# A shorter second key search, a 16-bit decoding, and GpSimd taken out of the low parts of U

## The chip, the cores and the metric

The kernel runs on one core of one Trainium2 chip. The metric is device time in microseconds (us), the median of several executions; lower is better. A core has TensorE (PE, matrix products; its weight loads are listed as PEld), VectorE (DVE), ScalarE (ACT), GpSimd (POOL), and SyncE (SP), which here issues the DMAs. Each engine works through its own queue in order and waits at semaphores for the others.

## The reference, cut to what matters

The model is a hybrid block (stick-breaking attention, a linear recurrence and an FFN) on 256 tokens of width 1024, followed by two layers of attention and an expert FFN, PEER. The change lies in PEER, which each of the two layers runs once:

```python
PEER_HEADS, PEER_NKEYS, PEER_TOPK = 8, 128, 16
q = (xc @ wq).reshape(PEER_CHUNK, PEER_HEADS, 2, half)
sc = jnp.einsum('chpd,hpnd->chpn', q, sub_keys)
s1, i1 = lax.top_k(sc[:, :, 0], PEER_TOPK)
s2, i2 = lax.top_k(sc[:, :, 1], PEER_TOPK)
cand = (s1[..., :, None] + s2[..., None, :])   # 16 x 16 sums
cidx = (i1[..., :, None] * PEER_NKEYS + i2[..., None, :])
top_s, pos = lax.top_k(cand, PEER_TOPK)        # over the 256 sums
eidx = jnp.take_along_axis(cidx, pos, axis=-1)
g = jax.nn.softmax(top_s, axis=-1)
a = gelu(u[eidx] . xc);  out = sum of (g * a) * v[eidx]
```

There are 16384 experts; u and v have 16384 rows of 1024 each.

## The kernel before, in words

The kernel does not gather the chosen rows. It multiplies all of U with all 256 tokens, block by block (128 blocks of 128 experts), and keeps the gelu of the products, `S`; it builds the gates of the chosen experts with one-hot matrices and multiplies them in; then it multiplies the gated `S` with all of V. In `peer` this is, in the order of the code:

- `query` (8 heads): W blocks are loaded, split and multiplied; ScalarE evicts the queries to `QT`.
- `topk(hd, t)` for 8 heads and two halves of the tokens (`t`): key scores by TensorE into `g`, copied to `sc`; then three searches for the best 16 on VectorE (`top16`, L1432 to L1436: the best 8, their places, take them out, the next 8, their places): one in each key half (128 scores), and, after the outer sum `cand` (L1451), one over the 256 sums, which gives values `tv` and places `pos`.
- `decode(t)`: a place is split into a = pos >> 4 and b = pos & 15; which key a or b stands for is found with a comparison against 0..15 (L1469), a product with the key numbers `ixf` (L1472) and a reduction (L1473), over 32 x 16 numbers of 32 bits, eight times for each half (two j, four x). Then the softmax: `gg` is the shifted `tv` (L1477), ScalarE takes its Exp (L1478), VectorE sums and divides; TensorE transposes, ScalarE and VectorE write `ID` and `GD`.
- `ublock(b)`: a block of U, 512 KB, comes by DMA into `raw` (3 buffers). A 32-bit number is split into a high part that TensorE takes as it is and a low part: ScalarE writes `hi` (L221), and `lo` = raw - hi (L222) is written by VectorE or GpSimd. There are two buffers of `hi`, two of `lo` and one more, `lo3`, for every third block. 24 matmuls follow (L1387, L1388 with `hi`, L1390 with `lo`) into one of two banks `a`, and ScalarE evicts it with a gelu (L1393, `S`). `uload` runs two blocks ahead.
- For the first `TURN` = 46 blocks, steps of `topk` and `decode` are put between the blocks: `steps()` yields 64 times, 14 of them during the queries and 50 over the 46 blocks.
- Afterwards `gstep` builds one-hots E of 8 tokens (L1527 to L1529) and multiplies (L1542), and the later blocks go on; then the V blocks (L1571).

Who makes `lo` is set by `ONPOOL`: every even block below 46 on GpSimd, 23 in a layer. The split is done by these lines of `load_split`:

```python
for a, b, r in parts:
    nc.scalar.activation(a, r, AF.Copy)
    (sub or nc.vector).tensor_sub(b, r, a.bitcast(F))
```

A scheduler orders each engine's queue by its own model of the times before the kernel is built, so the order on an engine is not that of the code.

Of the kernel before, what the change touches and what calls it, by code (L numbers as in the profile page):

```python
# [8 lines left out]
F = mybir.dt.float32  # L9
FR = mybir.dt.float32r  # L10
BF = mybir.dt.bfloat16
HF = mybir.dt.float16
U32 = mybir.dt.uint32
AF = mybir.ActivationFunctionType
OP = mybir.AluOpType
AX = mybir.AxisListType
# [1322 lines left out]


TURN = 46
ONPOOL = lambda b: b < TURN and b % 2 == 0


def peer(tc, A, K, dump, h, l, X, out):
    nc = tc.nc
    PSUM = bass.MemoryType.PSUM
    V, SC, G, PE = nc.vector, nc.scalar, nc.gpsimd, nc.tensor
    ident = K.ident
    ts = lambda t: slice(t * 128, (t + 1) * 128)  # L1350
    NT = 8

    def on_pool(b):
        return ONPOOL(b)

    with ExitStack() as es:
        pp = es.enter_context(tc.tile_pool(name=f"pp{l}", bufs=1))
# [13 lines left out]
        def uload(b):  # L1371

            def src(raw):
                nc.sync.dma_start(raw, A["peer_u_2"][l, b])

            room = pp.tile([128, 1024], FR, name="lo3", tag="lo3") if b % 3 == 2 else None
            hi, lo = K.load_split(src, 1024, lo=room, sub=G if on_pool(b) else None, halves=False)
            ub[b] = [x.rearrange("p (k e) -> p k e", k=8) for x in (hi, lo)]

        def ublock(b):  # L1380
# [13 lines left out]
            if n:  # L1394
# [4 lines left out]
        tp = tks.enter_context(tc.tile_pool(name=f"tp{l}", bufs=1))  # L1399
        iotaf = tp.tile([128, 128], F, name="iotaf")  # L1400
        G.iota(iotaf, [[1, 128]], base=0, channel_multiplier=0, allow_small_or_imprecise_dtypes=True)
        iota = iotaf[:, 0:16]
        V.tensor_copy(iotah, iotaf)
        QT = tp.tile([128, 8, 2, S], F, name="QT")
        KT = tp.tile([128, 8, 2, 128], F, name="KT")
        nc.scalar.dma_start(KT, A["peer_keys_2"][l])
        tk = [dict(tv=tp.tile([128, 8, 16], F, name=f"tv{t}"), pos=tp.tile([128, 8, 16], U32, name=f"pos{t}"),
                   ix=tp.tile([128, 8, 2, 16], U32, name=f"ix{t}")) for t in range(2)]
# [22 lines left out]
        def top16(v, ix, s, s2):  # L1431
            V.max(v[:, 0:8], s)  # L1432
            V.max_index(ix[:, 0:8], v[:, 0:8], s)
            V.match_replace(s2, v[:, 0:8], s, -3e38)  # L1434
            V.max(v[:, 8:16], s2)
            V.max_index(ix[:, 8:16], v[:, 8:16], s2)  # L1436

        def topk(hd, t):
            d = tk[t]
            w = pg.tile([128, 512], F, name="g", tag="g")  # L1440
            for j in range(2):
                PE.matmul(w[:, j * 128:(j + 1) * 128], lhsT=QT[:, hd, j, ts(t)], rhs=KT[:, hd, j], start=True, stop=True)
            v = tp.tile([128, 2, 16], F, name="v", tag="v", bufs=2)
            sc = tp.tile([128, 2, 128], F, name="sc", tag="sc", bufs=2)
            s2 = tp.tile([128, 256], F, name="s2", tag="s2", bufs=2)
            SC.activation(sc, w[:, 0:256].rearrange("p (j n) -> p j n", j=2), AF.Copy)
            for j in range(2):
                top16(v[:, j], d["ix"][:, hd, j], sc[:, j], s2[:, 0:128])
                yield
            cand = tp.tile([128, 256], F, name="cand", tag="cand", bufs=2)  # L1450
            V.tensor_add(cand.rearrange("p (a b) -> p a b", b=16), v[:, 0].unsqueeze(2).to_broadcast([128, 16, 16]),  # L1451
                         v[:, 1].unsqueeze(1).to_broadcast([128, 16, 16]))
            top16(d["tv"][:, hd], d["pos"][:, hd], cand, s2)
            yield

        def decode(t):
            d = tk[t]
            f = lambda nm: tp.tile([128, 8, 16], F, name=nm, tag=nm)
            u = tp.tile([128, 8, 16], U32, name="u", tag="u")
            ixf = tp.tile([128, 8, 2, 16], F, name="ixf", tag="ixf")  # L1460
            V.tensor_copy(ixf, d["ix"])
            sel = [f(f"sel{j}") for j in range(2)]
            for j in range(2):
                V.tensor_scalar(u, d["pos"], 4 if j == 0 else 15, None, op0=OP.logical_shift_right if j == 0 else OP.bitwise_and)
                pf = f("pf")
                V.tensor_copy(pf, u)
                for x in range(0, 8, 2):
                    oh = tp.tile([128, 32, 16], F, name="oh", tag="oh", bufs=2)
                    V.tensor_tensor(oh, pf[:, x:x + 2].rearrange("p h k -> p (h k)").unsqueeze(2).to_broadcast([128, 32, 16]),  # L1469
                                    iota.unsqueeze(1).to_broadcast([128, 32, 16]), op=OP.is_equal)  # L1470
                    o4 = oh.rearrange("p (h k) a -> p h k a", h=2)
                    V.tensor_mul(o4, o4, ixf[:, x:x + 2, j].unsqueeze(2).to_broadcast([128, 2, 16, 16]))  # L1472
                    V.tensor_reduce(sel[j][:, x:x + 2].rearrange("p h k -> p (h k)"), oh, AX.X, OP.add)  # L1473
                    if x < 6 or j == 0:
                        yield
            gg = f("gg")
            V.tensor_sub(gg, d["tv"], d["tv"][:, :, 0:1].to_broadcast([128, 8, 16]))  # L1477
            SC.activation(gg, gg, AF.Exp)  # L1478
# [5 lines left out]
            for j in range(2):  # L1484
                PE.transpose(w[:, j * 128:(j + 1) * 128], sel[j].rearrange("p h k -> p (h k)"), ident)
            PE.transpose(w[:, 256:384], gg.rearrange("p h k -> p (h k)"), ident)
            twice = lambda x: x.unsqueeze(len(x.shape)).to_broadcast(list(x.shape) + [2])
            SC.activation(ID[:, :, ts(t)], twice(w[:, 0:256].rearrange("p (j t) -> p j t", j=2)), AF.Copy)
            gs = tp.tile([128, 128], F, name="gs", tag="gs")
            SC.activation(gs, w[:, 256:384], AF.Copy, scale=2.0 ** 14)  # L1490
# [12 lines left out]
        done = 0  # L1503
# [150 lines left out]
```

## Time and profile before

| what | value |
|---|---|
| median of 3 runs | 2463.34 us (2461.76 to 2466.64) |
| the profiled execution | 2460.61 us, span 2458.8 us |
| TensorE busy | 2346.7 us, 95% |
| VectorE busy | 1697.5 us, 69% |
| ScalarE busy | 1205.5 us, 49% |
| GpSimd busy | 370.3 us, 15% |
| mean granted clock of TensorE | 0.982 of 2.4 GHz |

Busy times are shares of the whole span, which has many stages. What a stage is bound by is read from its own stretch: how much each engine is busy in it, what TensorE's idle time ended with, and at which clock it ran. 1.00 stands for 2.4 GHz and 0.50 for 1.2 GHz; a mean between them is a mix of the two over the stretch.

### The profile page before, as it was taken

The numbers are of one execution on the slowest core, as the hardware profiler recorded it, in microseconds if no ns is written. First come the engines' busy times: TensorE is split into PE (matmuls) and PEld (weight loads), VectorE is DVE, ScalarE is ACT, GpSimd is POOL, SyncE is SP. The second block draws the span as 40 slices with busy tenths as digits, with TensorE's granted clock in tenths as the row PEclk, the third lists the DMA queues.
The fourth block names the chain that finished last, engine by engine and source line by source line (L and its number), as shares of the span: only waits on it lengthen the run. The fifth ranks groups of instructions, "written<-read, shape, count | busy, mean of one in ns | idle before, by whom it ended". The sixth has DMA issues, their size and how long they took to land.

```text
span 2458.8 us, 43487 instructions
## 1 busy us (share of the span) xinstructions
PE 2346.7 (95%) x17012; PEld 2122.6 (86%) x17012; DVE 1697.5 (69%) x3190; ACT 1205.5 (49%) x2118; POOL 370.3 (15%) x299
## 2 busy tenths in 40 slices
PE   8978989998999999999999999999999999999998
PEld 7877879977799999999888877689999999888886
DVE  4467565557789968886555556779967888556555
ACT  4663554444435445544545454534545554455543
POOL 0065400007304410000000004502430000000000
PEclk9999999998999999999999999999999999999999
DMA  5332146555145454545556565325455555566664
GB/s 176 86 108 76 57 145 185 185 181 164 57 138 164 155 179 157 166 161 188 191 196 191 194 204 179 112 78 168 152 171 165 163 163 178 190 191 196 192 194 146
DMA packets 145637, 389.68 MB, mean 158 GB/s; under 512 B 18731, under 2 KB 49510, under 8 KB 145174
## 3 DMA queue, kind: packets, MB, share of 16 engines
q1 hardware_dynamic: 140070, 375.34, 47.8%
q10 hardware_dynamic: 5360, 11.56, 1.5%
q8 instruction: 133, 2.18, 0.4%
q14 instruction: 74, 0.61, 0.1%
HBM read 385.34 MB, written 1.31 MB: 157 GB/s over the span
## 4 chain that ended last, share of the span: by engine, by line
PE 56%; DVE 14%; issue 2%; ACT 2%; DMA 2%; POOL 0%; ACTq 0%; DVEq 0%; POOLq 0%
PE w L1571 27%; PE a L1387 7%; PE a L1388 7%; PE a L1390 7%; DVE lo L222 3%; PE w L1542 2%; PE a L1304 2%; DVE s L1434 1%; DMA raw<-in_peer_v_dram 1%; DVE oh L1469 1%; ACT hi L221 1%; PE w L1423 1%; PE o L1268 1%; DVE oh L1472 1%; DVE ix L1436 1%
## 5 line engine op out<-in xcount | busy, mean ns | idle before, releaser
L221 ACT ACTIVATE hi<-raw 128x1024 fp32r<-128x1024 f32 (+1 forms) x696 | 709.2, 1023 | 853.1 <-PE w L1571 312.0
L222 DVE TENSOR_TENSOR lo<-raw,hi 128x1024 fp32r<-128x1024 f32 (+1 forms) x610 | 745.7, 1224 | 524.6 <-ACT hi L221 518.9
L1387 PE MATMUL a<-XH,hi 128*128 128x256 f32 x2048 | 505.8, 285 | 8.9 <-ACT S L1393 5.9
L1388 PE MATMUL a<-XL,hi 128*128 128x256 f32 x2048 | 499.9, 282 | 0.0
L1571 PE MATMUL w<-hi,ww 128*128 128x512 f32 x1968 | 488.9, 389 | 4.1 <-ACT ww L226 4.1
L1571 PEld LDWEIGHTS w<-hi,ww 128*128 128x128 f32 x1968 | 368.8, 188 | 83.0 <-ACT ww L226 6.6
L1387 PEld LDWEIGHTS a<-XH,hi 128*128 128x128 f32 x2048 | 391.3, 191 | 12.7 <-ACT S L1393 6.3
L1388 PEld LDWEIGHTS a<-XL,hi 128*128 128x128 f32 x2048 | 391.3, 191 | 0.0
L1390 PE MATMUL a<-XH,lo 128*128 128x256 f32 x2048 | 293.2, 284 | 8.3 <-DVE lo L222 8.3
L1390 PEld LDWEIGHTS a<-XH,lo 128*128 128x128 f32 x2048 | 262.8, 190 | 9.3 <-DVE lo L222 9.1
L1571 PE MATMUL w<-lo,ww 128*128 128x512 f32 x984 | 264.4, 390 | 0.0
L222 POOL TENSOR_TENSOR lo<-raw,hi 128x1024 fp32r<-128x1024 f32 (+1 forms) x86 | 190.6, 2226 | 314.0 <-ACT hi L221 289.1
L173 POOL TENSOR_TENSOR ag<-ag,mhalf 128x1 f32<-128x1 f32 x10 | 9.5, 951 | 1464.0 <-DVE ag L349 1253.0
L1571 PEld LDWEIGHTS w<-lo,ww 128*128 128x128 f32 x984 | 184.2, 188 | 40.3 <-DVE lo L222 2.3
L264 PE MATMUL pj<-XH,hi 128*128 128x256 f32 (+1 forms) x424 | 124.6, 299 | 5.1 <-ACT gs L593 3.3
L266 PE MATMUL pj<-XH,lo 128*128 128x256 f32 (+1 forms) x424 | 117.5, 300 | 4.9 <-DVE lo L222 3.8
L265 PE MATMUL pj<-XL,hi 128*128 128x256 f32 (+1 forms) x424 | 122.1, 293 | 0.0
L227 DVE TENSOR_TENSOR ww<-S,ww 128x256 fp32r<-128x256 f32 x246 | 102.5, 417 | 0.0
L226 ACT ACTIVATE ww<-S 128x256 fp32r<-128x256 f32 x246 | 98.0, 399 | 0.0
L265 PE MATMUL pj<-big,hi 128*128 128x256 f32 x352 | 97.8, 283 | 0.0
L264 PE MATMUL pj<-big,hi 128*128 128x256 f32 x352 | 97.4, 283 | 0.0
L266 PE MATMUL pj<-big,lo 128*128 128x256 f32 x352 | 92.6, 283 | 0.0
(502 smaller groups left out, 3564.3 us busy)
## 6 DMA issues: line engine op xcount, KB each, us to landing
raw<-in_peer_u_dram SPq DMA_DIRECT2D x256, 512.0 KB
raw<-in_peer_v_dram SPq DMA_DIRECT2D x256, 512.0 KB
raw<-in_w_in_dram SPq DMA_DIRECT2D x58, 512.0 KB
raw<-in_w_ffn_in_dram SPq DMA_DIRECT2D x88, 256.0 KB
raw<-in_peer_wq_dram SPq DMA_DIRECT2D x32, 512.0 KB
raw<-in_w_ffn_out_dram SPq DMA_DIRECT2D x22, 512.0 KB
raw<-in_w_o_dram SPq DMA_DIRECT2D x16, 512.0 KB
raw<-in_w_out_dram SPq DMA_DIRECT2D x8, 512.0 KB
```

What stands on the lines that cost most here:

```text
L221: nc.scalar.activation(a, r, AF.Copy)
L222: (sub or nc.vector).tensor_sub(b, r, a.bitcast(F))
L226: self.nc.scalar.activation(hi, xf, AF.Copy)
L227: self.nc.vector.tensor_sub(lo, xf, hi.bitcast(F))
L264: PE.matmul(ps[j], lhsT=wh, rhs=xh(kk), start=kk == 0 and j % per == 0, stop=False)
L265: PE.matmul(ps[j], lhsT=wh, rhs=xl(kk), start=False, stop=False)
L266: PE.matmul(ps[j], lhsT=wl, rhs=xh(kk), start=False, stop=kk == KT - 1 and (j % per == per - 1 or j == len(subs) - 1))
L1304: K.marks["out"] = PE.matmul(po[t][c], lhsT=x[:, k, ts(t)], rhs=w[:, c * 512:(c + 1) * 512], start=f and not i and k == ks[0], stop=e and ...
L1387: PE.matmul(a, lhsT=hi[:, k], rhs=XH[:, k], start=k == 0, stop=False)
L1388: PE.matmul(a, lhsT=hi[:, k], rhs=XL[:, k], start=False, stop=False)
L1390: PE.matmul(a, lhsT=lo[:, k], rhs=XH[:, k], start=False, stop=k == 7)
L1571: K.marks["v"] = PE.matmul(acc[t][:, n], lhsT=x[:, ts(t)], rhs=v[:, n * 512:(n + 1) * 512], start=f, stop=e)
```

## The change

Three things change, all in `peer`. GpSimd makes no `lo` of U any more: `ONPOOL` and `on_pool` are gone, and VectorE makes all of them. The outer sums are cut to 112: the first four keys of one half with all 16 of the other, and the other twelve with the first four; a place is then decoded with a = max(pos >> 4, (pos >> 2) - 12) and b = pos - 16a + 12 max(a - 4, 0). The decoding works on all 8 heads at once, in 16-bit numbers: a comparison and a product over 8 x 16 x 16 = 2048 numbers, then a tree of additions instead of a reduction. `decode` yields 6 times instead of 8, so the steps are 60 and their pace over the blocks is set anew.

```diff
-ONPOOL = lambda b: b < TURN and b % 2 == 0
...
-            hi, lo = K.load_split(src, 1024, lo=room, sub=G if on_pool(b) else None, halves=False)
+            hi, lo = K.load_split(src, 1024, lo=room)
...
+        rank = tp.tile([128, 16, 16], HF, name="rank")
+        V.tensor_copy(rank, iota.unsqueeze(2).to_broadcast([128, 16, 16]))
...
-            cand = tp.tile([128, 256], F, name="cand", tag="cand", bufs=2)
-            V.tensor_add(cand.rearrange("p (a b) -> p a b", b=16), v[:, 0].unsqueeze(2).to_broadcast([128, 16, 16]),
-                         v[:, 1].unsqueeze(1).to_broadcast([128, 16, 16]))
-            top16(d["tv"][:, hd], d["pos"][:, hd], cand, s2)
+            cand = tp.tile([128, 112], F, name="cand", tag="cand", bufs=2)
+            for a, n, k in ((slice(0, 4), 4, 16), (slice(4, 16), 12, 4)):
+                V.tensor_add(cand[:, 16 * a.start:16 * a.start + n * k].rearrange("p (a b) -> p a b", b=k),
+                             v[:, 0, a].unsqueeze(2).to_broadcast([128, n, k]), v[:, 1, 0:k].unsqueeze(1).to_broadcast([128, n, k]))
+            top16(d["tv"][:, hd], d["pos"][:, hd], cand, s2[:, 0:112])
...
-            V.tensor_copy(ixf, d["ix"])
...
+            V.tensor_scalar(u, pos, 4, None, op0=OP.logical_shift_right)
+            V.tensor_scalar(u2, pos, 2, None, op0=OP.logical_shift_right)
+            V.scalar_tensor_tensor(ab[:, 0], u2, -12.0, u, op0=OP.add, op1=OP.max)
+            far, rest = f("far"), f("rest")
+            V.tensor_scalar(far, ab[:, 0], -4.0, 0.0, op0=OP.add, op1=OP.max)
+            V.scalar_tensor_tensor(rest, ab[:, 0], -16.0, pos, op0=OP.mult, op1=OP.add)
+            V.scalar_tensor_tensor(ab[:, 1], far, 12.0, rest, op0=OP.mult, op1=OP.add)
+            yield
             for j in range(2):
-                V.tensor_scalar(u, d["pos"], 4 if j == 0 else 15, None, op0=OP.logical_shift_right if j == 0 else OP.bitwise_and)
-                pf = f("pf")
-                V.tensor_copy(pf, u)
-                for x in range(0, 8, 2):
-                    oh = tp.tile([128, 32, 16], F, name="oh", tag="oh", bufs=2)
-                    V.tensor_tensor(oh, pf[:, x:x + 2].rearrange("p h k -> p (h k)").unsqueeze(2).to_broadcast([128, 32, 16]),
-                                    iota.unsqueeze(1).to_broadcast([128, 32, 16]), op=OP.is_equal)
-                    o4 = oh.rearrange("p (h k) a -> p h k a", h=2)
-                    V.tensor_mul(o4, o4, ixf[:, x:x + 2, j].unsqueeze(2).to_broadcast([128, 2, 16, 16]))
-                    V.tensor_reduce(sel[j][:, x:x + 2].rearrange("p h k -> p (h k)"), oh, AX.X, OP.add)
-                    if x < 6 or j == 0:
-                        yield
+                V.tensor_copy(ixd[:, j], twice(d["ix"][:, :, j]))
+                oh = tp.tile([128, 8, 16, 16], HF, name="oh", tag="oh", bufs=2)
+                V.tensor_tensor(oh, ab[:, j].unsqueeze(2).to_broadcast([128, 8, 16, 16]), rank.unsqueeze(1).to_broadcast([128, 8, 16, 16]),
+                                op=OP.is_equal)
+                yield
+                o4 = oh.rearrange("p h a (k u) -> p (h a) k u", u=2)
+                V.tensor_mul(o4, o4, ixd[:, j].rearrange("p h a u -> p (h a) u").unsqueeze(2).to_broadcast([128, 128, 8, 2]))
+                for n in (8, 4, 2):
+                    V.tensor_add(oh[:, :, 0:n], oh[:, :, 0:n], oh[:, :, n:2 * n])
+                V.tensor_add(sel[j], oh[:, :, 0], oh[:, :, 1])
+                yield
...
-            while done < 64 and done < 14 + (b + 1) * 50 // (TURN - 2):
+            while done < 60 and done < 14 + (b + 1) * 46 // (TURN - 2):
```

How the queues change is shown at three places of the first layer; a row is a line number, an operation, its tiles (numbers tell buffers of a name apart) and its shape. The first is GpSimd's queue from the number row `iotaf` on, before:

```order
L1401 IOTA iotaf 128x128
L222 TENSOR_TENSOR lo<-raw,hi 128x1024
L222 TENSOR_TENSOR lo_7233<-raw,hi 128x1024
L222 TENSOR_TENSOR lo<-raw,hi 128x1024 x2
L222 TENSOR_TENSOR lo_7473<-raw,hi 128x1024
L222 TENSOR_TENSOR lo<-raw,hi 128x1024 x2
L222 TENSOR_TENSOR lo_7720<-raw,hi 128x1024
```

and after:

```order
L1397 IOTA iotaf 128x128
L173 TENSOR_TENSOR ag<-ag,mhalf 128x1
L222 TENSOR_TENSOR big<-raw,big 128x512
L222 TENSOR_TENSOR big<-raw,big 128x256
L222 TENSOR_TENSOR big<-raw,big 128x512
L222 TENSOR_TENSOR big<-raw,big 128x256
L222 TENSOR_TENSOR big<-raw,big 128x512 x2
```

The `lo` of U are gone; the next thing GpSimd does is the layer norm's power and the weights of the second layer (`big`).

The second is VectorE's queue up to the softmax's `gg` of the first token half, before, from a `lo` on:

```order
L222 TENSOR_TENSOR lo<-raw,hi 128x1024
L1461 CAST ixf<-ix_6600 128x256
L1432 MAX tv_6598<-cand 128x8
L1433 MAX_INDEX pos_6599<-tv_6598,cand 128x8
L1434 MATCH_REPLACE s_8293<-tv_6598,cand 128x256
L1432 MAX v<-sc 128x8
L1435 MAX tv_6598<-s_8293 128x8
L1432 MAX v<-sc 128x8
L1433 MAX_INDEX ix_6603<-v,sc 128x8
L1434 MATCH_REPLACE s_8413<-v,sc 128x128
L1436 MAX_INDEX pos_6599<-tv_6598,s_8293 128x8
L1477 TENSOR_TENSOR gg<-tv_6598 128x128
```

and after, from the `lo` ahead of `gg` to the next one:

```order
L222 TENSOR_TENSOR lo_7844<-raw,hi 128x1024
L1433 MAX tv_6600<-s_8373 128x8
L1433 MAX tv_6603<-s_8494 128x8
L1434 MAX_INDEX pos_6601<-tv_6600,s_8373 128x8
L1488 TENSOR_TENSOR gg<-tv_6600 128x128
L1434 MAX_INDEX pos_6604<-tv_6603,s_8494 128x8
L1467 TENSOR_SCALAR u<-pos_6601 128x128
L1468 TENSOR_SCALAR u_8611<-pos_6601 128x128
L222 TENSOR_TENSOR lo<-raw,hi 128x1024
```

Before, `gg` stands twelve rows behind a `lo`, behind the cast `ixf`, and the last head of the second token half (the `sc` rows) is still in its first searches. After, the last search of both halves is nearly done at `gg`, the casts (`ixd`) stand further ahead, and the next `lo` follows four rows later.

The third is VectorE's queue in the decoding, before, around the `lo` that follows the first half's comparisons:

```order
L1469 TENSOR_TENSOR oh<-pf,iotaf 128x512 x2
L1472 TENSOR_TENSOR oh<-oh,ixf 128x512 x2
L1466 CAST pf<-u 128x128
L1473 TENSOR_REDUCE sel_8500<-oh 128x32
L222 TENSOR_TENSOR lo<-raw,hi 128x1024
L1473 TENSOR_REDUCE sel_8500<-oh 128x32
L1461 CAST ixf<-ix_6603 128x256
L1464 TENSOR_SCALAR u<-pos_6602 128x128
L1469 TENSOR_TENSOR oh<-pf,iotaf 128x512 x2
```

and after, at the first wide product:

```order
L222 TENSOR_TENSOR lo<-raw,hi 128x1024
L1482 TENSOR_TENSOR oh<-oh,ixd 128x2048
L1493 TENSOR_TENSOR gg<-gg,sm 128x128
L1478 TENSOR_TENSOR oh<-ab,rank 128x2048
L222 TENSOR_TENSOR lo_7965<-raw,hi 128x1024
L1484 TENSOR_TENSOR oh<-oh 128x8x128
L1482 TENSOR_TENSOR oh<-oh,ixd 128x2048
L1469 SCALAR_TENSOR_TENSOR ab<-u_8849,u 128x128
L222 TENSOR_TENSOR lo<-raw,hi 128x1024
L1484 TENSOR_TENSOR oh<-oh 128x8x64
L1484 TENSOR_TENSOR oh<-oh 128x8x128
```

Before, five or six rows (eight instructions, of 512 numbers most) stand between two `lo` of VectorE, and GpSimd makes the one between. After, every `lo` is here, with one to three wide or small operations between two.

## Rows read from the trace of the kernel before

**Rows 1.** Stretches: us, busy time (x instructions) by engine, PEclk, DMA share, GB/s.

```profile
683.10:864.90 181.80, 170.26 (x1386) 167.98 (x1387) 169.42 (x514) 85.77 (x135) 56.91 (x20) 0.96 0.48 158
1628.70:1811.50 182.80, 171.27 (x1438) 169.17 (x1439) 169.79 (x514) 85.60 (x135) 55.97 (x20) 0.96 0.49 158
683.10:735.00 51.90, 48.79 (x403) 47.47 (x404) 45.21 (x176) 21.93 (x37) 0.21 (x1) 1.00 0.45 150
735.00:788.70 53.70, 53.07 (x455) 52.87 (x454) 53.49 (x232) 28.09 (x44) 24.09 (x9) 1.00 0.55 177
788.70:864.90 76.20, 68.40 (x530) 67.65 (x531) 70.72 (x109) 35.75 (x54) 32.61 (x11) 0.91 0.46 150
1000.00:1100.00 100.00, 99.74 (x1117) 98.12 (x1117) 84.71 (x136) 49.52 (x106) 0.00 (x0) 1.00 0.50 164
```

**Rows 2.** Waits of TensorE, 683 to 865: total us, times, longest us.

```profile
PE a L1390 <- DVE lo L222: 4.2, 2, 2.3
PE a L1387 <- ACT S L1393: 3.0, 1, 3.0
...
PE w L1423 <- ACT hi L221: 1.0, 1, 1.0
```

**Rows 3.** Stretches around slow clock, columns as in rows 1.

```profile
790.00:798.00 8.00, 6.97 (x36) 6.97 (x37) 8.00 (x17) 3.63 (x6) 2.89 (x1) 0.57 0.43 133
820.00:826.00 6.00, 5.58 (x34) 5.58 (x35) 6.00 (x12) 2.32 (x3) 0.00 (x0) 0.72 0.47 175
848.00:852.00 4.00, 4.00 (x23) 4.00 (x23) 1.26 (x2) 0.96 (x2) 0.00 (x0) 0.57 0.85 292
```

**Rows 4.** Timeline: start us, us, engine, line, operation, tiles [idle before <-releaser].

```profile
782.56 3.15 POOL L222 TENSOR_TENSOR lo<-raw,hi 128x1024 fp32r<-128x1024 f32 x1 [2.43 <-ACT hi L221]
783.36 2.50 DVE L1461 CAST ixf<-ix 128x256 f32<-128x256 uint32 x1
785.46 1.28 ACT L1478 ACT_TABLE_LOAD   x1
788.98 0.31 ACT L1478 ACTIVATE gg<-gg 128x128 f32<-128x128 f32 x1 [2.24 <-DVE gg L1477]
789.30 1.28 ACT L1393 ACT_TABLE_LOAD   x1
791.03 0.58 PE L1387 MATMUL a<-XH,hi 128*128 128x256 f32 x1 [2.96 <-ACT S L1393]
...
816.91 2.38 POOL L222 TENSOR_TENSOR lo<-raw,hi 128x1024 fp32r<-128x1024 f32 x1 [2.77 <-ACT hi L221]
817.15 3.22 DVE L222 TENSOR_TENSOR lo<-raw,hi 128x1024 fp32r<-128x1024 f32 x1
```

**Rows 5.** VectorE by form, 735 to 788.7: xcount | busy us, mean ns.

```profile
L222 DVE TENSOR_TENSOR lo<-raw,hi 128x1024 fp32r<-128x1024 f32 x8 | 9.6, 1206 | 0.0
...
L1436 DVE FIND_INDEX8 ix<-v,s 128x8 uint32<-128x128 f32 x18 | 5.0, 282 | 0.0
L1451 DVE TENSOR_TENSOR cand<-v 128x256 f32<-128x256 f32 x9 | 4.9, 543 | 0.0
L1436 DVE FIND_INDEX8 pos<-tv,s 128x8 uint32<-128x256 f32 x11 | 4.5, 415 | 0.0
```

**Rows 6.** VectorE by form, 788.7 to 864.9.

```profile
L222 DVE TENSOR_TENSOR lo<-raw,hi 128x1024 fp32r<-128x1024 f32 x12 | 18.3, 1526 | 0.6 <-issue 0.6
L1472 DVE TENSOR_TENSOR oh<-oh,ixf 128x512 f32<-128x512 f32 x16 | 14.9, 966 | 0.0
L1469 DVE TENSOR_TENSOR oh<-pf,iotaf 128x512 f32<-128x512 f32 x16 | 14.9, 959 | 0.0
L1473 DVE TENSOR_REDUCE sel<-oh 128x32 f32<-128x512 f32 x16 | 10.4, 673 | 0.0
...
L1529 DVE TENSOR_TENSOR E<-E,GD 128x1024 f16<-128x1024 f16 x2 | 1.3, 677 | 0.0
```

**Rows 7.** VectorE by form, 885 to 1100.

```profile
L1396 DVE TENSOR_TENSOR S<-a,S 128x64 f32<-128x64 f32 x2 | 0.4, 215 | 0.0
```

More of the change, by code (lines that the diff above doesn't have):

```diff
@@ L1351, in peer @@
     NT = 8
-    def on_pool(b):
-        return ONPOOL(b)
     with ExitStack() as es:
@@ L1458, in decode @@
             f = lambda nm: tp.tile([128, 8, 16], F, name=nm, tag=nm)
-            u = tp.tile([128, 8, 16], U32, name="u", tag="u")
-            ixf = tp.tile([128, 8, 2, 16], F, name="ixf", tag="ixf")
-            V.tensor_copy(ixf, d["ix"])
-            sel = [f(f"sel{j}") for j in range(2)]
-            for j in range(2):
-                V.tensor_scalar(u, d["pos"], 4 if j == 0 else 15, None, op0=OP.logical_shift_right if j == 0 else OP.bitwise_and)
-                pf = f("pf")
-                V.tensor_copy(pf, u)
-                for x in range(0, 8, 2):
-                    oh = tp.tile([128, 32, 16], F, name="oh", tag="oh", bufs=2)
-                    V.tensor_tensor(oh, pf[:, x:x + 2].rearrange("p h k -> p (h k)").unsqueeze(2).to_broadcast([128, 32, 16]),
-                                    iota.unsqueeze(1).to_broadcast([128, 32, 16]), op=OP.is_equal)
-                    o4 = oh.rearrange("p (h k) a -> p h k a", h=2)
-                    V.tensor_mul(o4, o4, ixf[:, x:x + 2, j].unsqueeze(2).to_broadcast([128, 2, 16, 16]))
-                    V.tensor_reduce(sel[j][:, x:x + 2].rearrange("p h k -> p (h k)"), oh, AX.X, OP.add)
-                    if x < 6 or j == 0:
-                        yield
@@ new lines, in decode @@
+            twice = lambda x: x.unsqueeze(len(x.shape)).to_broadcast(list(x.shape) + [2])
+            pos = d["pos"]
+            u, u2 = (tp.tile([128, 8, 16], U32, name=n, tag=n) for n in ("u", "u2"))
+            ab = tp.tile([128, 2, 8, 16], HF, name="ab", tag="ab")
+            ixd = tp.tile([128, 2, 8, 16, 2], HF, name="ixd", tag="ixd")
+            sel = [f(f"sel{j}") for j in range(2)]
+            V.tensor_scalar(u, pos, 4, None, op0=OP.logical_shift_right)
+            V.tensor_scalar(u2, pos, 2, None, op0=OP.logical_shift_right)
@@ L1486, in decode @@
             PE.transpose(w[:, 256:384], gg.rearrange("p h k -> p (h k)"), ident)
-            twice = lambda x: x.unsqueeze(len(x.shape)).to_broadcast(list(x.shape) + [2])
             SC.activation(ID[:, :, ts(t)], twice(w[:, 0:256].rearrange("p (j t) -> p j t", j=2)), AF.Copy)
```

## The prediction

> **What bounds the kernel now.** I read the page's totals first, then the stretches, then what TensorE waits for, then what those waits rest on. TensorE is busy in nearly all of the span, so only places where it stands still or runs slow can give time back. In each of the two expert layers there is one such place: from the first query projection to the first gating matmul, 683.1 to 864.9 us and 1628.7 to 1811.5 us [rows 1]. The reader is to see TensorE's busy time, its clock and VectorE's busy time together. After that place, from 1000 to 1100, TensorE is busy 99.74 of 100 us although VectorE is busy 84.71 [rows 1]: one `lo` per U block on VectorE with this much beside it holds nobody up. Inside the place TensorE is idle 181.80 - 170.26 = 11.5 us and its clock is 0.96.
>
> The idle time has names [rows 2]: 4.2 us until a `lo` of VectorE, in two waits; 3.0 us until a gelu of ScalarE (`S`), in one wait; the rest, 4.3 us, is the first loads of the queries and the first one-hots E. Behind each of the three long waits the granted clock falls to its half level for a while: 0.57 over 8 us, 0.72 over 6 us, 0.57 over 4 us [rows 3]. That costs 8 x 0.43 + 6 x 0.28 + 4 x 0.43 = 3.4 + 1.7 + 1.7 = 6.8 us more. So 11.5 + 6.8 = 18.3 us of a layer's 181.8 are lost, and 1628.7 to 1811.5 has the same sums (11.5 us idle, clock 0.96). All of it won twice would be 37 us, the ceiling.
>
> What the waits rest on is in the timeline [rows 4]. At 816.91 GpSimd starts a `lo` of 2.38 us; at 817.15 VectorE starts one, and it takes 3.22 us where the same shape has a mean of 1.206 in a stretch where none of its eight was stretched [rows 5]. TensorE waits for exactly this one. At 783.36 a cast of 256 numbers takes 2.50 us, again beside a GpSimd `lo`; five us later ScalarE's Exp has waited 2.24 us for VectorE's `gg`, which stands behind that cast, and ScalarE's queue is in order, so the gelu behind the Exp and its table load (1.28 us) is late and TensorE waits 2.96 us for a free bank. The shift is seen in the means too: between 788.7 and 864.9 `lo` has 1526 ns, the decoding's product and comparison 966 and 959, but the reduction of as many elements 673 [rows 6].
>
> **The change, part by part.** Everything is for one layer; both layers have it.
>
> *GpSimd's 23 `lo` go to VectorE* (20 of them in this place, 9 and 11 in its two later stretches [rows 1]). VectorE pays 20 x 1.206 = 24.1 us. It gets back what the overlap cost it: 12 x (1.526 - 1.206) + 16 x (0.966 - 0.673) + 16 x (0.959 - 0.673) = 3.8 + 4.7 + 4.6 = 13.1 us in the decoding, and 9 x (0.543 - 0.43) + 2.50 - 0.28 = 3.2 us in the search (0.28 is the price of a 128-element operation [rows 5], 0.43 that of two adds of 64 [rows 7]). The Trainium skill, "SBUF — State Buffer", section "Who interferes with whom", says that VectorE and GpSimd share one port pair as a lock, held for a whole instruction, and that the one issued second stops altogether. The 3.22 us beside 1.206 agree; by the rule alone each of the 20 operations could block VectorE for all of its 2.4 us, 48 us in all, VectorE would be free of its backlog, and the time would be that of the second rival below.
>
> *The second search over 112 sums.* An index search takes 415 ns over 256 elements and 282 over 128 [rows 5], 1.04 ns an element; 144 fewer save 0.15 us, and the five passes of a search 0.75 us. Two adds of 64 and 48 instead of one of 256 cost 0.43 us or less, against 0.543 beside GpSimd: nothing more is counted. 16 searches save 12 us, 9 of them after the queries: 6.7 us.
>
> *Decoding.* Before, 16 times three operations of 512 elements: 16 x 3 x 0.673 = 32.3 us without the overlap's cost. After, for each of two halves: twice a comparison and a product of 2048 16-bit numbers, a tree of 1024, 512 and 256 and a last add, six small operations, two casts. The trace has no such operation of 2048. 1024 16-bit numbers take 677 ns, as 512 of 32 bits do (673) [rows 6], so two 16-bit numbers pass in the time of one, and 2048 should cost the 1.21 us of a `lo`. At one number a pass it would be 0.28 + 1920 x 0.00104 = 2.28 us. I take 1.21, the nearer row, and for the tree 0.68 + 0.42 + 0.28 + 0.28. A half costs 2 x (2.42 + 1.66) + 8 x 0.28 = 10.4 us, a layer 20.8: 11.5 us less. At the upper price it would be some 12 us more than that.
>
> *What of it is on the path.* Two stretches have to be told apart.
>
> In the search, 735 to 788.7, VectorE is busy 53.49 of 53.70 us and TensorE 53.07 [rows 1]: they are at par, so here VectorE's balance is what counts. The nine `lo` come in: +10.9. The nine searches save 6.7, the overlap 3.2. But the order now puts the last head's searches of the second token half ahead of `gg` (the rows of the order above): some nine short operations of 0.28 us, 2.5 us more in front of it. Balance +3.5 us: in this stretch VectorE gets later, not earlier. The 0.6 us in which TensorE already stands still there cover a part, and I count 2.9 us of new, short waits for `lo`.
>
> In the decoding, 788.7 to 864.9, VectorE is busy 70.72 us. It loses 13.1 + 11.5 + 2.5 and takes on 11 x 1.206 = 13.3: 56 us. TensorE needs 68.40 - 6.8 of slow clock = 61.6. Here VectorE has room, no `lo` is stretched, and both long waits with the half clock behind them go: 4.2 + 1.7 + 1.7 = 7.6 us.
>
> The wait for the gelu: without the 2.50 us cast `gg` is no longer 2.24 us late, but ScalarE still loads two tables and does an Exp between two evictions, so of 2.96 us about 1.0 stays. I take 2.0 us back, and the 3.4 us of half clock behind it, since the wait left is no longer than the 1.0 us of the query stretch [rows 2], in which the clock stays at 1.00 [rows 1]. Together 5.4.
>
> First loads and one-hots: as before. The new `rank` cast falls before the queries, beside TensorE's warming matmuls: nothing.
>
> Sum of a layer: -7.6 - 5.4 + 2.9 = -10.1 us; two layers -20. GpSimd, now idle here, gives nothing by itself. The profiled execution took 2460.61 us (span 2458.8); 2440.4 comes of it. The median of the runs is 2463.34, 2.7 above the profiled one, so I predict 2443.
>
> **Rivals.**
>
> *The gelu wait stays.* VectorE is as late at `gg` as before, since its balance in the search is +3.5 us, the saved cast's 2.2 included. Then only -7.6 + 2.9 = -4.7 a layer: 2463.3 - 9.4 = 2454. For it: 53.49 of 53.70. Against it: the lateness, 2.24 us, is almost exactly what the one stretched cast costs.
>
> *VectorE does not run behind at all.* The order has a `lo` after every six to eight short operations, and what these overlap may be worth more than I took off. Then nothing is added: 13.0 a layer, 2463.3 - 26 = 2437. With the query waits gone too it would be 2426, the ceiling.
>
> *VectorE becomes the bound, and it gets slower.* Place: the search, where one queue now holds every `lo` behind up to eight search operations. If the 112-element passes save nothing (if they are fixed cost), 6.7 us are added to the 2.9: 9.6 us of waits, some long enough for two more half-clock stretches of 1.7, and the gelu wait stays. A layer: -7.6 + 9.6 + 3.4 = +5.4; 2474. It decides from about 5 us of balance on. Against it: 415 and 282 ns, which differ by the elements. The Trainium skill, "Perfetto Trace Analysis", section "Optimizing Scalar/DVE Operations", advises to move work off a saturated VectorE, even to GpSimd, and adds that between these two it may not help because of a shared port; the first half speaks for this rival, the 3.22 us row for the second half.
>
> *No change.* The wide operations at 2.28 us: decoding 56 + 12 = 68 us for TensorE's 61.6, some 6 us a layer of waits again, and the clock with them (3.4): 2463.3 - 20 + 19 = 2462.
>
> **How the numbers follow.** Forecast 0.43, gelu wait stays 0.22, VectorE not behind 0.22, no change 0.07, slower 0.06. The likeliest alone would lie between 2437 and 2449. For 8 in 10 the range takes in the first two rivals with some room: 2430 to 2457. A change under 0.2% (4.9 us) cannot be told from none: 2458.4 and 2468.3 are the bounds. From the forecast and the second rival all, from the first most of it is faster: 0.84; same 0.10 (no change, the slow end of the first rival); slower 0.06.
>
> **What would show it.** Right: no GpSimd subtraction in this place; `lo` near 1.21 us throughout; TensorE's waits for `lo` many and under 1 us; clock 1.00 from the search to the one-hots; the gelu wait near 1 us; index searches over 112 near 0.27 us; the 2048-wide operations near 1.2; the first gating matmul about 10 us earlier after the first query than now. Wrong: a wait of 2 us or more at the Exp with a slow clock behind it; wide operations near 2.3 us; VectorE without a pause up to the one-hots; or the same stretch lengthened by waits for `lo` in the search.

## The result, and the profile after

The changed kernel takes 2433.09 us (median of 4, 2431.37 to 2437.14) against 2462.55 us beside it: ratio 0.9889, interval 0.9877 to 0.9901. The forecast of 2443 had the direction; the gain is 29.5 us and not 20.

The stretches after, with the columns of [rows 1]. The first two rows are the place of each layer from the first query projection to the first gating matmul, the others its three parts:

```profile
684.80:848.00 163.20, 161.21 (x1367) 159.98 (x1368) 145.65 (x531) 85.01 (x134) 0.00 (x0) 1.00 0.54 174
1617.00:1780.20 163.20, 161.30 (x1367) 159.88 (x1368) 145.73 (x531) 84.97 (x134) 0.00 (x0) 1.00 0.54 174
...
684.80:736.70 51.90, 50.68 (x425) 49.89 (x426) 45.28 (x212) 22.70 (x39) 0.00 (x0) 1.00 0.48 155
736.70:788.00 51.30, 51.27 (x440) 51.07 (x439) 51.30 (x242) 27.63 (x44) 0.00 (x0) 1.00 0.56 180
788.00:848.00 60.00, 59.26 (x507) 59.02 (x506) 49.07 (x79) 34.68 (x52) 0.00 (x0) 1.00 0.57 185
```

The place ends after 163.2 us instead of 181.2. The queue of TensorE has 14 matmuls fewer in it (they come later), 1.6 us; the other 16.4 us are idle time (11.2 to 2.0 us) and clock (0.96 to 1.00). In the fourth row VectorE is busy all the time, as it was before, and TensorE has 0.03 us of idle time. TensorE's waits in the first row (total us, times, longest), all there are, for [rows 2]:

```profile
PE w L1421 <- DVE lo L222: 1.2, 4, 0.5
PE a L1383 <- ACT S L1389: 0.7, 1, 0.7
```

The chain of [rows 4] after (start us, us, engine, line, operation, tiles, idle before):

```profile
783.28 0.28 DVE L1476 CAST ixd<-ix 128x256 f16<-128x256 uint32 x1
...
787.62 1.28 ACT L1489 ACT_TABLE_LOAD   x1
787.69 0.26 DVE L1488 TENSOR_TENSOR gg<-tv 128x128 f32<-128x128 f32 x1
...
788.92 0.31 ACT L1489 ACTIVATE gg<-gg 128x128 f32<-128x128 f32 x1
789.25 1.28 ACT L1389 ACT_TABLE_LOAD   x1
...
790.98 0.39 PE L1383 MATMUL a<-XH,hi 128*128 128x256 f32 x1 [0.74 <-ACT S L1389]
```

The cast of 256 numbers takes 0.28 us (2.50 before), `gg` is there during the table load, the Exp waits for nothing, and 0.74 us of the 2.96 are left: two table loads and an Exp. VectorE by form in the search, 736.7 to 788, for [rows 5] (x count | busy us, mean ns):

```profile
L222 DVE TENSOR_TENSOR lo<-raw,hi 128x1024 fp32r<-128x1024 f32 x18 | 21.6, 1202 | 0.0
...
L1431 DVE FIND_INDEX8 pos<-tv,cand 128x8 uint32<-128x112 f32 x10 | 2.6, 260 | 0.0
...
L1452 DVE TENSOR_TENSOR cand<-v 128x64 f32<-128x64 f32 x8 | 1.6, 197 | 0.0
L1452 DVE TENSOR_TENSOR cand<-v 128x48 f32<-128x48 f32 x8 | 1.5, 186 | 0.0
```

and in the decoding, 788 to 848, for [rows 6]:

```profile
L222 DVE TENSOR_TENSOR lo<-raw,hi 128x1024 fp32r<-128x1024 f32 x21 | 25.6, 1218 | 9.5 <-ACT hi L221 9.4
L1482 DVE TENSOR_TENSOR oh<-oh,ixd 128x2048 f16<-128x2048 f16 x4 | 4.8, 1212 | 0.0
L1478 DVE TENSOR_TENSOR oh<-ab,rank 128x2048 f16<-128x2048 f16 x4 | 4.8, 1211 | 0.0
L1484 DVE TENSOR_TENSOR oh<-oh 128x1024 f16<-128x1024 f16 x4 | 2.7, 678 | 0.0
```

`lo` is at 1.20 to 1.22 us, the search over 112 at 0.26, the 2048-wide operations at 1.21, and VectorE now pauses 9.4 us for `hi`: it is no longer late there.

Where the 29.2 us of the span went, by stage (from the starts of the first query, first V matmul, and last V matmul in each trace):

| stage | before, us | after, us | difference |
|---|---|---|---|
| up to the first query | 683.1 | 684.8 | +1.7 |
| layer 1, first query to first V block | 468.8 | 451.7 | -17.1 |
| V blocks of layer 1 | 351.6 | 351.5 | -0.1 |
| between the layers | 125.3 | 129.0 | +3.7 |
| layer 2, first query to first V block | 468.6 | 451.8 | -16.8 |
| from there to the end | 361.4 | 360.8 | -0.6 |

The two expert layers give 33.9 us; 4.7 of them are missing again outside, in stages of which the change rewrites no line. The end of the experiments comes back to them.

### The profile page after: what moved, and what is told of

Read it like the earlier page. It is cut to its first block, busy times and chain, and to the rows that moved or that the text cites. A ratio compares the mean times of both kernels' runs of the same rounds, so it can differ in the third digit from the quotient of the medians.

```text
span 2429.6 us, 43499 instructions
## 1 busy us (share of the span) xinstructions
PE 2334.9 (96%) x17012; PEld 2111.7 (87%) x17012; DVE 1662.0 (68%) x3234; ACT 1204.5 (50%) x2118; POOL 241.5 (10%) x253
## 3 DMA queue, kind: packets, MB, share of 16 engines
q10 hardware_dynamic: 5360, 11.56, 1.5%
## 4 chain that ended last, share of the span: by engine, by line
PE 74%; DVE 7%; issue 4%; ACT 2%; DMA 2%; POOL 1%; DVEq 0%; ACTq 0%; POOLq 0%
PE w L1581 27%; PE a L1383 10%; PE a L1384 10%; PE a L1386 9%; PE pj L302 3%; PE w L1552 2%; PE pj L264 2%; PE pj L266 2%; DVE lo L222 2%; PE pj L265 2%; PE a L1304 2%; PE w L1421 1%; ACT hi L221 1%; DMA raw<-in_peer_v_dram 1%; PE o L1268 1%
## 5 line engine op out<-in xcount | busy, mean ns | idle before, releaser
L222 DVE TENSOR_TENSOR lo<-raw,hi 128x1024 fp32r<-128x1024 f32 (+1 forms) x656 | 792.6, 1210 | 543.0 <-ACT hi L221 540.0
L1383 PE MATMUL a<-XH,hi 128*128 128x256 f32 x2048 | 498.4, 283 | 2.5 <-ACT S L1389 1.5
L1384 PE MATMUL a<-XL,hi 128*128 128x256 f32 x2048 | 492.4, 280 | 0.0
L1383 PEld LDWEIGHTS a<-XH,hi 128*128 128x128 f32 x2048 | 385.3, 188 | 6.4 <-DVE S L1392 3.6
L1384 PEld LDWEIGHTS a<-XL,hi 128*128 128x128 f32 x2048 | 385.9, 188 | 0.0
L1386 PE MATMUL a<-XH,lo 128*128 128x256 f32 x2048 | 287.1, 281 | 0.0
L1389 ACT ACTIVATE S<-a 128x256 f32<-128x256 f32 (+18 forms) x248 | 75.7, 305 | 30.2 <-PE a L1386 30.1
```

Source lines behind the costliest of these rows:

```text
L1383: PE.matmul(a, lhsT=hi[:, k], rhs=XH[:, k], start=k == 0, stop=False)
L1384: PE.matmul(a, lhsT=hi[:, k], rhs=XL[:, k], start=False, stop=False)
L1386: PE.matmul(a, lhsT=lo[:, k], rhs=XH[:, k], start=False, stop=k == 7)
L1389: SC.activation(o[:, n:], a[:, n:], AF.Gelu)
```

## The experiments

Two theories were set against each other. Overlap: VectorE loses time to GpSimd's operations that run beside its own, and taking them away is what gains. Work: VectorE has less to do with the shorter search and decoding, and who makes the low parts is indifferent. As the stages outside differ by some us from kernel to kernel, the layers are compared too: all times "a layer" go from the first query to the first V block, layer 1 / layer 2. Each ratio is to runs of the kernel before made beside that kernel.

| kernel | median, us | ratio to before, interval | a layer, us |
|---|---|---|---|
| before | 2462.55 | 1 | 468.8 / 468.6 |
| only GpSimd's low parts to VectorE | 2444.52 | 0.9928 (0.9904 to 0.9952) | 455.3 / 455.3 |
| low parts and the 16-bit decoding (old search) | 2432.69 | 0.9879 (0.9855 to 0.9903) | 454.9 / 454.0 |
| low parts and the search over 112 (old decoding) | 2432.83 | 0.9887 (0.9870 to 0.9903) | 451.6 / 451.7 |
| all three, the changed kernel | 2433.09 | 0.9889 (0.9877 to 0.9901) | 451.7 / 451.8 |
| search and decoding, GpSimd as before | 2467.56 | 1.0025 (1.0014 to 1.0037) | 469.4 / 467.6 |
| changed, ten low parts a layer made twice | 2460.34 | 0.9993 (0.9983 to 1.0004) | 464.9 / 467.1 |
| changed, all 23 low parts a layer made twice | 2479.21 | 1.0065 (1.0044 to 1.0087) | 474.1 / 475.7 |
| changed, 23 copies a layer by GpSimd | 2447.89 | 0.9945 (0.9929 to 0.9962) | 462.7 / 455.4 |
| changed, ten copies a layer by GpSimd | 2439.52 | 0.9909 (0.9892 to 0.9925) | 453.2 / 454.3 |

**Only GpSimd's low parts moved.**

```diff
-ONPOOL = lambda b: b < TURN and b % 2 == 0
+ONPOOL = lambda b: False
```

> The kernel before, with GpSimd's 46 low parts of U given to VectorE and nothing else: the search over 256 and the 32-bit decoding stay. Overlap theory (VectorE loses its time to GpSimd's operations beside it): VectorE gets 16 us a layer back and takes on 24, so 169 + 8 = 177 us of work in a place that lasts 182; no operation is stretched any more and the half clock behind the long waits goes, but the waits become many small ones: 2452 to 2466. Work theory (the gain comes from the shorter search and decoding; who makes the low parts is indifferent): 24 us more a layer on an engine that is the bound in the search already: 2480 to 2500.

Measured 2444.52. The work theory falls; the overlap theory holds and asked for too little. 13.4 of the 17 us a layer come from this line alone, although VectorE has the old search and the old decoding to do. The stretches (place and search):

```profile
684.10:883.40 199.30, 195.42 (x1657) 193.91 (x1657) 186.03 (x545) 101.30 (x159) 0.00 (x0) 1.00 0.52 174
...
736.00:789.70 53.70, 53.70 (x463) 53.70 (x463) 53.70 (x204) 28.33 (x46) 0.00 (x0) 1.00 0.54 177
```

In the search VectorE and TensorE are both busy in 53.70 of 53.70 us: nobody waits. What VectorE cannot do there it does later: the first gating matmul comes after 1657 matmuls, not 1381, some eleven U blocks on, and that delays nothing, since U blocks fill the time. TensorE's waits in the place:

```profile
PE w L1423 <- ACT hi L221: 1.0, 1, 1.0
PE a L1387 <- ACT hi L221: 1.0, 1, 1.0
PE w L1423 <- DVE lo L222: 0.9, 2, 0.6
PE a L1387 <- ACT S L1393: 0.7, 1, 0.7
```

The two waits for `hi` stand in the kernel before too (one of them in [rows 2]); no wait for a `lo` of U is left. The median gains only some 17 us of the 26.8 that the two layers give, because 9 us are lost between the layers; the end of this section shows that stage.

**Search and decoding without that.** The changed kernel, with GpSimd's part put back:

```diff
-            hi, lo = K.load_split(src, 1024, lo=room)
+            hi, lo = K.load_split(src, 1024, lo=room, sub=nc.gpsimd if ONPOOL(b) else None, halves=False)
```

> The changed kernel with GpSimd's low parts as before (every even block below 46), the search over 112 and the 16-bit decoding kept. Overlap theory: single low parts and wide 16-bit operations still take 2 to 3.5 us beside GpSimd, and TensorE still has waits above 1 us with a half clock behind them: 2443 to 2455. Work theory: VectorE has 12 us of search and 11.5 us of decoding less in each layer and no low part more, so it is never late: 2430 to 2436, no slower than the changed kernel.

Measured 2467.56, slower than before by 0.14 to 0.37%; the layers are as before. Both theories missed: I had half the gain in mind. VectorE is busy 1665.7 us in all for 1697.5, some 16 us less a layer, and none of it helps while GpSimd stands beside it. The scheduler's order is another one here too: the first gating matmul comes after 1139 matmuls, not 1381, so it is the layers, which hold the same work, that are compared. TensorE's waits in layer 1's place:

```profile
PE a L1387 <- DVE lo L222: 10.2, 5, 2.4
PE a L1384 <- ACT S L1390: 2.8, 2, 2.4
PE w L1422 <- DVE lo L222: 1.2, 4, 0.5
```

Behind these stands, as before, a wait of 0.96 us for the first one-hot E. VectorE's products into E take up to 2.89 us beside a `lo` of GpSimd in this run, and 0.69 at most without one; with only the low parts moved, the wait is gone.

**The second search over 256 again, and the old decoding again.** Each is one part of the changed kernel undone, with the places decoded to match. The first, from the changed kernel:

```diff
-            cand = tp.tile([128, 112], F, name="cand", tag="cand", bufs=2)
+            cand = tp.tile([128, 256], F, name="cand", tag="cand", bufs=2)
...
-            V.tensor_scalar(u2, pos, 2, None, op0=OP.logical_shift_right)
+            V.tensor_scalar(u2, pos, 15, None, op0=OP.bitwise_and)
+            V.tensor_copy(ab[:, 0], u)
+            V.tensor_copy(ab[:, 1], u2)
```

and the second, from the kernel before:

```diff
-ONPOOL = lambda b: b < TURN and b % 2 == 0
+ONPOOL = lambda b: False
...
-            cand = tp.tile([128, 256], F, name="cand", tag="cand", bufs=2)
+            cand = tp.tile([128, 112], F, name="cand", tag="cand", bufs=2)
...
+            V.scalar_tensor_tensor(pa, u2, -12.0, u, op0=OP.add, op1=OP.max)
+            V.tensor_scalar(far, pa, -4.0, 0.0, op0=OP.add, op1=OP.max)
+            V.scalar_tensor_tensor(pb, pa, -16.0, pos, op0=OP.mult, op1=OP.add)
+            V.scalar_tensor_tensor(pb, far, 12.0, pb, op0=OP.mult, op1=OP.add)
```

> The changed kernel with the second search over all 256 sums again (16-bit decoding kept, GpSimd makes no low part). It prices the search: 12 us more of VectorE a layer, 6.7 of them after the queries, where VectorE has no pause. Overlap theory: no operation is stretched, but low parts come late in the search: 3 to 7 us of waits a layer, 2440 to 2448. Work theory: half of the saved work is gone and the low parts are there: 2450 to 2465. If the search had slack for it: 2433 to 2436.

> The kernel before with VectorE making all low parts and with the search over 112, but the old 32-bit decoding. It prices the decoding: 11.5 us less of VectorE a layer in the changed kernel, in a stretch where VectorE has pauses. Theory: that work is hidden, so the same time as the changed kernel or up to 2 us more a layer (0.8 was the difference with the search over 256): 2432 to 2437. Rival: the decoding ends later and the waits for the low parts come back: 2438 to 2445.

Measured 2432.69 and 2432.83: neither is told apart from the changed kernel, and in the second run the theory holds. In the first, the median is that of its third case, slack in the search (0.3 us below it). Only the layers show a price: in them the decoding is worth nothing (451.65 without, 451.75 with it) or 0.85 us (455.3 to 454.45, with the old search), and the search 2.7 us with the new decoding (454.45 to 451.75), 3.65 with the old one. The 11.8 us between the medians of the first run and of the low parts alone are not the decoding's work: in the profiles 8.7 of them lie between the layers (134.4 and 125.7 us). Some 1.7 of the search's 2.7 us are seen in the waits of the kernel with 256:

```profile
PE w L1421 <- ACT hi L221: 1.0, 1, 1.0
PE a L1383 <- ACT hi L221: 1.0, 1, 1.0
PE w L1421 <- DVE lo L222: 0.9, 2, 0.6
PE a L1383 <- ACT S L1389: 0.7, 1, 0.7
```

The two waits of 1.0 us for `hi`, in and behind the queries, stand in every kernel with the search over 256 and in none with 112. By what way the shorter search removes them was not followed further. No wait for a `lo` of U came with the longer search.

**The low parts made twice.** In the changed kernel, behind `load_split`:

```diff
+            if b < TURN and b % 2 == 0:
+                jk = tp.tile([128, 1024], FR, name="junk", tag="junk")
+                G.tensor_sub(jk, raws[b], hi.bitcast(F))
```

> The changed kernel, in which GpSimd makes the low part of every even U block below 46 a second time, into a tile that nobody reads: VectorE's work and order stay as in the changed kernel, only GpSimd's 23 operations a layer stand beside them again. Overlap theory: low parts and wide operations of VectorE beside them take 2 us and more, VectorE loses up to 16 us a layer, of which its 10 us of pauses in the decoding take some: 2438 to 2455. Work theory: nobody waits for GpSimd, so 2431 to 2437.

> The changed kernel, in which GpSimd makes the low part a second time, into a tile that nobody reads, only for the ten even U blocks below 20 of each layer: these stand beside the search, and the order of every other engine is the changed kernel's, row for row. Overlap theory: passes of the search keep their 0.26 to 0.28 us beside GpSimd, but low parts and sums of VectorE wait for the end of its operation, up to 2.3 us each, and TensorE behind them with a half clock after it: 5 to 10 us a layer, 2445 to 2458. Slack theory (same overlap, but between two low parts the order leaves VectorE the room): 2434 to 2440. Work theory: 2431 to 2437 and no operation longer.

With all 23 a layer 2479.21, 46 us slower than the changed kernel, slower than before, and above the range of the overlap theory (ratio 1.0065, 1.0044 to 1.0087). In that run the gating also comes nine U blocks later (1583 matmuls before it, not 1367), so its order is not the changed kernel's. The second run (`b < 20`, 2460.34, 2 us above the overlap theory's range) is clean of that: TensorE, VectorE, ScalarE and the DMAs have the changed kernel's order row for row. Ten operations a layer that nobody reads cost it 13.2 and 15.3 us, 1.4 us for each, and give back nearly the whole gain. The timeline shows how:

```profile
740.74 2.40 POOL L1377 TENSOR_TENSOR junk<-raw,hi 128x1024 fp32r<-128x1024 f32 x1 [3.28 <-ACT hi L221]
742.10 2.12 DVE L222 TENSOR_TENSOR lo<-raw,hi 128x1024 fp32r<-128x1024 f32 x1
744.27 1.21 PE L1390 MATMUL a<-XH,lo 128*128 128x256 f32 x8 [0.54 <-DVE lo L222]
...
768.08 2.39 POOL L1377 TENSOR_TENSOR junk<-raw,hi 128x1024 fp32r<-128x1024 f32 x1 [3.21 <-ACT hi L221]
769.33 2.22 DVE L222 TENSOR_TENSOR lo<-raw,hi 128x1024 fp32r<-128x1024 f32 x1
771.60 1.21 PE L1390 MATMUL a<-XH,lo 128*128 128x256 f32 x8 [1.68 <-DVE lo L222]
...
777.44 2.41 POOL L1377 TENSOR_TENSOR junk<-raw,hi 128x1024 fp32r<-128x1024 f32 x1 [6.98 <-ACT hi L221]
777.46 0.28 DVE L1438 FIND_INDEX8 ix<-v,s 128x8 uint32<-128x128 f32 x1
777.66 2.39 DVE L1456 TENSOR_TENSOR cand<-v 128x64 f32<-128x64 f32 x2
```

GpSimd's operation ends at 743.14; VectorE's `lo`, begun at 742.10, ends 1.08 us after that and not 1.2 after its start. That fits a `lo` that stood still for 1.04 us and then took nearly its own time. All eight `lo` that begin beside a subtraction in this run end 1.08 us behind it. The same sum fits before [rows 4]: GpSimd ends at 816.91 + 2.38 = 819.29, VectorE's `lo` at 817.15 + 3.22 = 820.37, again 1.08 later. At 777.46 an index search passes beside GpSimd in its usual 0.28 us, and the two adds behind it, of 64 and 48 sums, take 2.39 us, where such a pair takes 0.31: the first ends 0.08 us after GpSimd. So it is operations with two inputs, and casts like the one of [rows 4], that can stop; the search does not. The Trainium skill, "SBUF — State Buffer", section "Who interferes with whom", says that a VectorE instruction with at most one input from SBUF, outside the two-port modes, does not contend with GpSimd; the 0.28 us agrees. TensorE's waits in this place:

```profile
PE a L1390 <- DVE lo L222: 6.5, 5, 2.1
PE a L1387 <- ACT S L1393: 3.3, 2, 2.9
PE g L1444 <- ACT sc L1448: 1.8, 1, 1.8
PE w L1425 <- DVE lo L222: 1.1, 4, 0.5
```

One thing the run mixes in: `junk` also reads `raw` and `hi` and so keeps their buffers longer. ScalarE waits 1.5 us for it once, and it waits for late loads three times in the first layer, 4.5 us in all, and twice in the second, 3.9. A GpSimd operation that reads neither was not tried.

**A copy in place of the subtraction.** `G.tensor_copy(jk, raws[b])`, all 23 and then the ten below 20, the second again with the order of the changed kernel on the other engines.

> As the run with the low parts made twice (all 23 even blocks below 46), but GpSimd's operation is a copy of raw, with one input in place of two. If every operation of GpSimd holds VectorE back, by its length: operations of 64 to 256 numbers on VectorE stretch to the copy's length, and with a copy of 1.2 to 2.4 us the time is 2445 to 2480. If only an operation with two inputs does: no operation is stretched and the time is 2432 to 2440.

> The changed kernel, in which GpSimd copies raw (one input) into a tile that nobody reads, for the ten even U blocks below 20 of each layer; again the order of every other engine is the changed kernel's, row for row. The same with the two-input subtraction measured 2460. If a GpSimd operation holds VectorE back by its length whatever its form, the copy of 1.6 us for the subtraction's 2.65 costs 12 to 17 us: 2445 to 2450. If only two-input operations hold it back: 2431 to 2437. The 46 copies of the earlier run cost 15 us, a third of a us each; 20 such would give 2438 to 2441.

Measured 2447.89 and 2439.52. GpSimd's copy takes 1.04 us undisturbed, the subtraction 2.38 to 2.41. Neither rule fits: ten copies cost 1.5 and 2.5 us a layer, 0.2 us for each, so one input is not free (one `lo` beside a copy took 1.76 us, one add of 48 took 0.84), but it costs a seventh of the subtraction and not its half. The copies keep `raw` too, and ScalarE waits for late loads about as long (3.5 us in the first layer, 6.1 in the second), so this buffer by itself explains little of the subtraction's price. What holding `hi` costs beyond that one wait of 1.5 us is not separated. In the longer run something else came up: GpSimd can starve.

```profile
800.61 12.66 POOL L1377 CAST junk<-raw 128x1024 fp32r<-128x1024 f32 x2 [5.14 <-DMA raw<-in_peer_u_dram]
```

The row joins two copies: the first takes 11.56 us, the second 1.04. During the first VectorE runs sums, products, low parts and casts of the decoding one behind the other. `raw` is held so long that a load comes late (ScalarE waits 7.6 us for it) and TensorE waits 6.6 us in one piece.

**The changed kernel again, and the lesson carried to other stages.** `vrec` gives the recurrence's 40 low parts to VectorE, `vatt` those of the two attentions:

```diff
-                          lambda j, ps, g=g: SC.activation(dst[:, 4 * g + j], ps, AF.Sigmoid), pj, sub=G))
+                          lambda j, ps, g=g: SC.activation(dst[:, 4 * g + j], ps, AF.Sigmoid), pj, sub=V))
```

> The changed kernel, and in the recurrence of the first layers GpSimd's 40 low parts of 512 are VectorE's too (same halves). Carried-over theory: TensorE waits 5.6 us for these low parts of GpSimd (1.5 us each, 0.7 on VectorE), and VectorE's operations beside them are no longer stretched: 2424 to 2431. Rival: there VectorE has its own chain, low parts stand in line behind it, and what GpSimd loses TensorE waits for at VectorE: 2433 to 2442.

> The changed kernel, and in both attentions GpSimd's low parts of the weights (56 of 256 to 512 numbers) are VectorE's too (same halves). Carried-over theory: single operations of VectorE there are stretched beside GpSimd and TensorE's waits for them (3.8 us for RP in the second layer) go: 2426 to 2432. Rival: VectorE is busy 7 to 10 of 10 us there and the low parts come late: 2434 to 2445.

> The changed kernel itself, as the base for the other runs beside it: 2431 to 2437. Its second profile is to tell what the unchanged stages (ahead of the first queries, and between the two layers) do by themselves: if the 1.7 and 3.7 us that they were longer in the first profile are chance, they are other numbers here, while the two expert layers stay within 0.5 us of 451.7 and 451.8.

> The changed kernel with the recurrence's 40 low parts on VectorE, beside the changed kernel on the same chip. Carried-over theory: 2 to 5 us faster than the changed kernel, all of it ahead of the first queries (680.3 us up to them in its first profile). Chance theory: within 1 us of it.

The recurrence: 2430.17, and beside the changed kernel 2431.72 (2427.80 to 2436.53) against 2434.12 (2430.34 to 2436.04). Up to the first query it has 680.3 and 682.1 us against 684.8 and 684.9, but over the whole time 2.4 us between ranges that overlap are not shown. TensorE's 5.6 us of waits for GpSimd's low parts went, and its waits for VectorE's rose from 3.5 to 9.2 and 7.4. The attentions: 2437.68 (2434.07 to 2444.73), no gain; the rival was nearer. Where VectorE is in the chain itself, the trade is about even. The repeat of the changed kernel shows layers of 451.7 / 451.7 and the same 684.9 and 128.9 us in the stages outside: so the 4.7 us are not chance of one execution of the changed kernel.

Ahead of the first query every engine has the same order in the kernels of the table's first six rows, and the time goes from 682.9 to 687.8 us; the 1.7 us between before and after lie inside that, and their cause stays open. Between the layers the instructions are the same but the scheduler's order is not. Before and the old search (with the new decoding) have one order in every engine's queue, 125.3 and 125.7 us. The changed kernel, the old decoding, and the run with GpSimd as before have a second, 129.0, 128.8 and 128.7. The low parts alone have a third, 134.4 at a clock of 0.92. The stage before, after, and with the low parts alone:

```profile
1503.50:1628.80 125.30, 113.74 (x676) 90.76 (x675) 91.87 (x206) 59.55 (x157) 62.86 (x66) 0.97 0.35 113
...
1488.00:1617.00 129.00, 113.72 (x677) 91.38 (x675) 92.93 (x208) 59.37 (x157) 64.02 (x66) 0.97 0.33 110
...
1492.20:1626.60 134.40, 118.87 (x677) 95.83 (x675) 93.93 (x206) 59.12 (x157) 64.45 (x66) 0.92 0.32 106
```

In the second order TensorE has a wait in the attention that the first does not have, for a tile `RP` of VectorE; after:

```profile
PE a L1218 <- DVE RP L1213: 3.8, 2, 3.4
```

The same order gives the same time within 0.4 us, and so the 3.7 us go with the second order and the 9 us with the third. No run changed the order of this stage by itself, so more than that is not shown.

## Why the prediction was right or wrong

*What bounds the kernel.* Right: the whole gain is in the two places named. Their loss of 18.3 us a layer was called the ceiling, and nearly all of it (16.4, and 17 up to the V blocks) came.

*Long waits for `lo` and the clock behind them, -7.6.* Right: 4.2 us of waits are gone and the clock is 1.00. The reason is shown by three runs: one line that removes GpSimd's operations removes the waits, putting ten of them back brings waits back, and shortening VectorE's work beside them (in an order of its own) does nothing.

*The gelu wait, -5.4.* Right, mechanism and size: 2.96 to 0.74 us (1.0 was forecast), no slow clock behind it, the cast at 0.28.

*Costs.* `lo` at 1.21, 260 ns for a search over 112 (0.27 forecast), 1.21 us for 2048 16-bit numbers instead of the upper 2.28: right. But the decoding's 11.5 us and most of the search's 12 were never on the path; they were put there only through the balance of the next step.

*New short waits in the search, +2.9 a layer.* This step failed. It read "they are at par, so here VectorE's balance is what counts", and took 3.5 us of balance for 2.9 us of waits. There were none, and even 24 us more of low parts with the old search and decoding brought none (both engines busy in 53.70 of 53.70 us). That fits a VectorE that is full because every gap between two low parts is filled with search work that nobody waits for yet; more work makes the search end later, not the next `lo`. The second rival ("does not run behind at all") had the result, with 0.22, but its reason was that the overlap is worth more; what the runs show is that the lateness had no taker.

*First loads and one-hots, "as before".* Failed, smaller: 2.7 us a layer. Two waits of 1.0 us in and behind the queries went with the shorter search, as the runs with 256 show (`lo` waits there grew by 0.3), and the 1.0 us wait for the first one-hot went too, that one with GpSimd's operations and not with the search. I had counted nine of sixteen searches "after the queries" and left the seven among them without a price.

*The sum.* -7.6 - 5.4 + 2.9 = -10.1 was forecast; -7.6 - 5.6 + 0 - 2.7 = -15.9 came of the same terms, and 16.4 at equal matmuls. That the time is only 10 us off is partly luck: 4.7 us went again outside the layers, 3.7 of them with a new order between the layers that the prediction did not look at. A slip in it changes nothing: VectorE's 56 us of work in the decoding are 56.9 by its own terms (70.72 - 27.1 + 13.3).

*Rivals.* VectorE as the bound, a staying gelu wait, and no change by wide operations at 2.28 are all refuted by the rows above.

## What to carry to other kernels

An engine that is busy in 100% of a stretch is late only if somebody waits for it: read the waits of the bounding engine, and look whether the busy engine's work has a due time or merely fills gaps. Work handed to GpSimd is not free for VectorE: a two-input operation there stopped VectorE's adds, products and casts for up to the rest of its length (2.4 us here), so compare the duration of the same form with and without a neighbour before calling an offload a relief. Where one operation is stretched, add GpSimd's end and the operation's own time: if the sum is near its end, it stood still for GpSimd. Before a difference in a stage that was not edited is put down to chance, compare the order of its queues.

## What the runs showed that was not expected

- Ten GpSimd subtractions a layer that nobody reads cost 28 us in all, as much as the change gained; ten copies cost 4.
- The loss goes both ways: GpSimd's low parts of U beside VectorE took up to 4.2 us instead of 2.4 in the kernel before, the low parts made twice up to 10.1 (23 a layer), and one of the 23 copies 11.56 instead of 1.04.
- A half clock does not follow every wait of some 2 us. With the ten subtractions TensorE waits 11.6 us between 736.6 and 861.1, in pieces of up to 2.9, and the clock of the place stays at 1.00; in the second layer there is one stretch of 3.4 us at the half level, at 1751, and the mean is 0.99:

```profile
684.70:861.10 176.40, 163.58 (x1366) 160.66 (x1366) 157.90 (x531) 85.30 (x134) 26.51 (x10) 1.00 0.48 161
1629.50:1808.10 178.60, 165.49 (x1366) 162.23 (x1366) 160.44 (x531) 85.44 (x134) 25.61 (x10) 0.99 0.48 159
```

  So the 6.8 us that before lost to the clock [rows 3] are not simply the price of waits of that length.
